# A WKV recurrence on one Trainium2 core: both ends of a written-out order are placed anew

## The chip, the cores and the metric

The kernel runs on one core of one Trainium2 chip. A core has five engines that follow their own instruction queues: TensorE (PE, matrix products into PSUM), VectorE (DVE), ScalarE (ACT), GpSimd (POOL) and SyncE (SP, used here for transfers only). The metric is the device time of the kernel in microseconds; less is better.

## The reference

For each of 16 sequences and 256 channels a state runs over 2048 time steps. It is kept with a running maximum so that no exponential overflows:

```python
for t in range(seq_len):
    ww = u + kk;      qq = maximum(pp, ww)
    e1 = exp(pp - qq); e2 = exp(ww - qq)
    output[b, t] = (e1 * aa + e2 * vv) / (e1 * bb + e2 + 1e-08)
    ww = pp - w + kk; qq = maximum(ww, kk)
    e1 = exp(ww - qq); e2 = exp(kk - qq)
    aa = e1 * aa + e2 * vv; bb = e1 * bb + e2; pp = qq
```

Inputs: w and u (256), k and v (16 x 2048 x 256), all fp32; the output is 16 x 2048 x 256 fp32.

## The kernel before

Time is cut into 16 chunks of 128 steps (c = 0 to 15), the batch into 4 groups of 4 sequences. One group in one chunk is a *pair* n = 4c + p, 64 in all; its k and its v are 512 KB each, its output too. Within a chunk everything is a product with a triangular matrix over time, so TensorE does the sums over time and the state is handed over from chunk to chunk by a short chain on small tiles.

A pair goes through these steps. The engine is in brackets, then the line of the program; q is 0 or 1.

- LK, LV (GpSimd's or SyncE's transfers, L108, L111, L115): loads of k and v. RK (VectorE or GpSimd, L194) copies k to the matmul type, CV (L214) casts v to bf16.
- R q (TensorE, L201, 4 products) and L q (TensorE, L207, 2 products) build the logarithms in one of two PSUM buffers X[0], X[1]; X q (ScalarE, L210) takes their exponential into a ring of 11 pairs, EZR.
- TV (VectorE, L219) multiplies by v. S (TensorE, L246, 8 products) sums over time into TOT.
- DEN (TensorE, L323, 12 products into X) and NUM (the same into a buffer of its own, or into X for the odd ones of the last eight pairs) give the denominator and numerator. LN (ScalarE, L335) and INV (ScalarE, L340) turn the denominator into its inverse, MUL (VectorE, L355) makes the output, ST (SyncE, L368, L361) and SQ store it.

After the S of a chunk's four pairs comes the chain of the state: CS (VectorE, L252, copies the sums), TU (TensorE, L259, turns them into TOT's other columns), SL (ScalarE, L263, logarithm), FR and OF (VectorE, L268 to L276), SW (ScalarE, L282), CH (VectorE, L286, L289), SS (VectorE, L296), TK (TensorE, L303, turns back into TURN), BK (VectorE, L307, copies it). DEN and NUM of the chunk's pairs need BK. SN (L279) and KP (L299) hand two tiles to the next chunk.

The order is written out by the program itself. Each step gets a place, a number: by default the pair's number plus a constant of the table P, in which pair n's output follows about 10 pairs behind its input. The table AT gives single steps a place of their own. At each turn the step with the lowest place whose predecessors are written and whose buffer is free is written; every engine then does its own instructions in that order, and the waits between engines follow from the tiles.

```python
ops[name] = dict(place=AT.get(key, place), fn=fn, args=args, after=list(after), take=take, give=give, mode=mode)
...
todo = sorted(ops, key=lambda x: ops[x]["place"])
```

Fillers: ahead of some TensorE steps a number of products with zeros into TURN is written (`zeros`, L149). Before the first step there are 26. Table Z0 counts them for the steps whose number is 0 and Z for all others; none is written between a TK and its BK, as BK reads TURN. With "L": 1 each L has one.

```python
if o["mode"] and not quiet:
    zeros(P["Z0" if name[-1] < FILL else "Z"].get(name[0], 0))
quiet = quiet and name[0] != "BK" or name[0] == "TK"
```

Buffers that matter here: X[0] and X[1], shared by R/L/X and by DEN/LN; one buffer for NUM; two for the inverse; 4 and 5 for k, 4 for v, 2 for its cast; 8 for the output.

Of the kernel before, what the change touches and what calls it, by code (L numbers as in the profile page):

```python
# [15 lines left out]
def kernel(  # L16
# [37 lines left out]
    FILL = 1  # L54
# [4 lines left out]
         "R": [-0.795, -7.965],  # L59
         "OUT": {"DEN": [-0.47, -0.155, -0.55, -0.495], "LN": [-11.935, -9.86, -0.84, -6.17], "INV": [-13.87, -8.32, -4.99, -5.82], "NUM": [-0.105, 0.155, 0.11, -5.15], "MUL": [1.115, 0.345, 0.895, 1.035], "ST": [-5.05, 7.26, 1.245, 7.765], "SQ": [-3.365, 6.69, -2.4, 8.84]},  # L60
         "TAIL": {"DEN": -4.36, "LN": -16.54, "INV": 3.8, "NUM": -0.31, "MUL": 4.39, "ST": 14.35, "step": 2.989, "SQ": 26.08},
         "Z0": {"L": 1, "S": 3, "DEN": 0, "NUM": 6, "TK": 47, "TU": 17, "R": 12},
         "Z": {"DEN": 0, "L": 1, "NUM": 0, "TK": 4, "S": 0, "TU": 1, "R": 0}}

    AT = {"INV 55": 69.0, "SL 15": 69.1, "LN 56": 69.2, "SW 15": 75.7, "FR 15": 69.3}

    consts = ctx.enter_context(tc.tile_pool(name="consts", bufs=1))
    kpool = ctx.enter_context(tc.tile_pool(name="kpool", bufs=NK))
# [63 lines left out]
    Z = consts.tile([128, 192], BF16, tag="Z", name="Z")  # L132
# [14 lines left out]
    def zeros(m, first=False):  # L147
        for j in range(m):
            K(PE.matmul(TURN[:, 0:192], Z[:, 0:128], Z, start=first, stop=True, skip_group_check=True))  # L149
# [40 lines left out]
    X = [psx.tile([128, 2, D], F32, tag=f"X{a}", name=f"X{a}") for a in range(2)]  # L190
# [31 lines left out]
    AS, D1, L1, A0, FR, BC, A2 = range(7)  # L222
# [88 lines left out]
    RD, NUM, OT = {}, {}, {}  # L311
# [66 lines left out]
    def step(name, place, fn, args=(), after=(), take=None, give=(), mode=0):  # L378
        key = name if isinstance(name, str) else " ".join(map(str, name))
        ops[name] = dict(place=AT.get(key, place), fn=fn, args=args, after=list(after), take=take, give=give, mode=mode)  # L380

# [51 lines left out]
    while todo:  # L433
        for name in todo:
            o = ops[name]
            if all(x not in ops or "done" in ops[x] for x in o["after"]) and (xs if o["take"] == "X" else free.get(o["take"], 1)):
                break
        else:
            raise AssertionError(todo[:9])
        todo.remove(name)  # L440
        args = list(o["args"])
        if o["take"] == "X":
            held[name] = xs.pop(0)
            args.append(held[name])
        elif o["take"]:
            free[o["take"]] -= 1
        elif name[0] == "L":
            args.append(held[("R",) + name[1:]])
        for g in o["give"]:
            if g == "X":  # L450
                x = held[("DEN", name[1]) if name[0] == "LN" else ("NUM", name[1]) if name[0] == "MUL" else ("R",) + name[1:]]
                xs.append(x)
                args.append(x)
            else:
                free[g] += 1
        if o["mode"] and not quiet:
            zeros(P["Z0" if name[-1] < FILL else "Z"].get(name[0], 0))
        quiet = quiet and name[0] != "BK" or name[0] == "TK"
        o["fn"](*args)
        o["done"] = True  # L460
# [30 lines left out]
```

## Time and profile before

| | |
|---|---|
| median of 3 runs | 289.46 us (288.67 to 289.91) |
| the profiled execution | 289.20 us, span 287.5 us |
| TensorE busy | 271.6 us, 94% |
| ScalarE busy | 258.6 us, 90% |
| VectorE busy | 246.9 us, 86% |
| GpSimd busy | 176.4 us, 61% |
| fillers (L149) | 319 products, 11% of the chain that ended last |
| moved | 101.2 MB, 67.12 read and 33.55 written, 350 GB/s over the span |

Busy time counts an engine's instructions from start to modelled end; products overlap, so a busy TensorE need not be at its peak. What an engine waited for stands in brackets behind the first instruction after the wait. Times in the rows are microseconds from the start of the span.

### The profile page before, as it was taken

How to read it: one execution, taken by the hardware profiler on the slowest of the kernel's cores; microseconds unless marked ns; L12 is line 12 of the kernel's file. 1: busy time of each engine (PE TensorE's matmuls, PEld its weight loads, DVE VectorE, ACT ScalarE, POOL GpSimd, SP SyncE). 2: the span in 40 equal slices, each digit the busy share in tenths (PEclk: the TensorE clock that was granted, in tenths of full speed). 3: DMA queues.
4: the chain of work that ended last, by engine and by line, in shares of the span. 5: the costliest groups of instructions: out<-in, count | busy, mean ns of one | idle time of the engine just before them, and what ended most of it. 6: DMA issues, size and time to landing. Idle time of an engine off the chain costs nothing.

```text
span 287.5 us, 8058 instructions
## 1 busy us (share of the span) xinstructions
PE 271.6 (94%) x3263; PEld 139.2 (48%) x3263; DVE 246.9 (86%) x422; ACT 258.6 (90%) x291; POOL 176.4 (61%) x219
## 2 busy tenths in 40 slices
PE   7989999999999999999999999999999999998860
PEld 6535744454545545454545545454545545454530
DVE  4685879989897979989898989989898989889861
ACT  1776399999999999999999999999999999998991
POOL 8256458575767687575767687575767685421320
PEclk9999999999999999999999999999999999999997
DMA  6999999999999999999999999999999999985896
GB/s 206 348 354 346 347 348 313 384 369 390 374 394 381 383 393 372 391 382 393 355 392 388 389 387 382 394 385 395 370 380 374 389 394 387 347 237 177 235 278 179
DMA packets 58669, 101.20 MB, mean 352 GB/s; under 512 B 5152, under 2 KB 43688, under 8 KB 58632
## 3 DMA queue, kind: packets, MB, share of 16 engines
q0 software_dynamic: 21200, 65.42, 65.5%
q1 hardware_dynamic: 37280, 35.14, 36.4%
q8 instruction: 25, 0.41, 0.6%
q10 hardware_dynamic: 152, 0.14, 0.1%
q14 instruction: 12, 0.10, 0.1%
HBM read 67.12 MB, written 33.55 MB: 350 GB/s over the span
## 4 chain that ended last, share of the span: by engine, by line
PE 81%; ACT 6%; DMA 4%; DVE 4%; issue 2%; SPq 1%; DVEq 0%; ACTq 0%
PE X L207 20%; PE X L323 15%; PE num L323 12%; PE X L201 12%; PE TURN L149 11%; PE TOT L246 7%; DMA ot<-in_v_dram 4%; ACT rd L335 3%; PE TOT L259 2%; DVE ot L355 2%; ACT rd L340 2%; DVE EZR L219 1%; ACT EZR L210 1%; PE TURN L303 1%; SPq L115 1%
## 5 line engine op out<-in xcount | busy, mean ns | idle before, releaser
L210 ACT ACTIVATE EZR<-X 128x1024 bf16<-128x1024 f32 x128 | 126.9, 1014 | 14.4 <-PE X L207 14.2
L214 POOL CAST vb<-vr 128x1024 bf16<-128x1024 f32 x54 | 56.4, 1044 | 69.3 <-DVE EZR L219 67.5
L219 DVE TENSOR_TENSOR EZR<-EZR,vb 128x2048 bf16<-128x2048 bf16 x64 | 77.8, 1219 | 0.4 <-ACT EZR L210 0.2
L355 DVE TENSOR_TENSOR ot<-num,rd 128x1024 f32<-128x1024 f32 x60 | 73.3, 1221 | 3.9 <-ACT rd L340 3.6
L340 ACT ACTIVATE rd<-rd 128x1024 f32<-128x1024 f32 (+1 forms) x65 | 68.0, 1046 | 2.0
L335 ACT ACTIVATE rd<-X 128x1024 f32<-128x1024 f32 (+1 forms) x65 | 65.8, 1012 | 2.3 <-PE X L323 0.7
L149 PE MATMUL TURN<-Z 128*128 128x192 bf16 x319 | 55.2, 259 | 1.4 <-DVE Z L133 1.4
L201 PE MATMUL X<-WU,CO 64*64 64x512 bf16 x512 | 51.9, 390 | 0.9 <-DVE WU L176 0.6
L149 PEld LDWEIGHTS <-Z 128*128 128x128 bf16 x319 | 28.4, 100 | 48.6 <-issue 47.1
L115 POOL DMA_DIRECT2D vr<-in_v_dram x61 | 46.3, 759 | 6.7 <-DVE vb L214 5.9
L207 PE MATMUL X<-kr,NLE 128*128 128x512 f32 x128 | 45.6, 438 | 0.0
L207 PE MATMUL X<-kr,NLZ 128*128 128x512 f32 x128 | 45.5, 437 | 0.0
L108 POOL DMA_DIRECT2D kf<-in_k_dram x53 | 40.1, 756 | 0.0
L194 DVE CAST kr<-kf 128x1024 fp32r<-128x1024 f32 x39 | 31.6, 839 | 4.0 <-DMA kf<-in_k_dram 4.0
L201 PEld LDWEIGHTS <-CO 64*64 64x64 bf16 x512 | 15.7, 105 | 31.1 <-issue 26.3
L323 PE MATMUL X<-EZR,S 64*64 64x512 bf16 x256 | 26.2, 394 | 1.7 <-ACT rd L335 1.0
L323 PE MATMUL X<-cb,Id 64*64 64x512 bf16 x256 | 25.9, 376 | 0.0
L323 PE MATMUL X<-EZR,Id 64*64 64x512 bf16 x256 | 25.9, 376 | 0.0
L323 PE MATMUL num<-EZR,SN 64*64 64x512 bf16 x240 | 24.3, 386 | 1.1 <-DVE ot L355 1.1
L246 PE MATMUL TOT<-EZR,OH 128*32 128x256 bf16 x512 | 23.7, 277 | 1.3 <-DVE EZR L219 1.3
L323 PE MATMUL num<-cb,IdN 64*64 64x512 bf16 x240 | 24.0, 376 | 0.0
L323 PE MATMUL num<-EZR,IdN 64*64 64x512 bf16 x240 | 23.9, 376 | 0.0
(69 smaller groups left out, 269.3 us busy)
## 6 DMA issues: line engine op xcount, KB each, us to landing
vr<-in_v_dram POOLq DMA_DIRECT2D x61, 512.0 KB, 7.7
kf<-in_k_dram POOLq DMA_DIRECT2D x53, 512.0 KB, 8.5
out_dram<-ot SPq DMA_DIRECT2D x64, 256.0 KB, 10.0
out_dram<-ot SPq DMA_DIRECT2D x116, 128.0 KB, 10.1
kr<-in_k_dram POOLq DMA_DIRECT2D x8, 512.0 KB, 8.8
ot<-in_k_dram SPq DMA_DIRECT2D x3, 512.0 KB, 5.9
ot<-in_v_dram SPq DMA_DIRECT2D x3, 512.0 KB, 10.0
out_dram<-ot POOLq DMA_DIRECT2D x11, 128.0 KB, 3.4
```

What stands on the lines that cost most here:

```text
L115: K((SP if n < BYSP else POOL).dma_start(out=vr, in_=rows_of(v, n)))
L149: K(PE.matmul(TURN[:, 0:192], Z[:, 0:128], Z, start=first, stop=True, skip_group_check=True))
L201: K(PE.matmul(X[a][o:o + HS, i, :].rearrange("p (n d) -> p n d", n=2), CO[r:r + HS, q, :], WU[r:r + HS, :].unsqueeze(1).broadcast_to([HS, ...
L207: K(PE.matmul(X[a][:, i, :], (NLE, NLZ)[q], km[:, i, :], start=False, stop=True, skip_group_check=True))
L210: K(SC.activation(ez(n)[:, q, 1], X[a], ACT.Exp))
L214: K((DVE if n < EARLY else POOL).tensor_copy(vb, VR.pop(n)))
L219: K(DVE.tensor_mul(ez(n)[:, :, 0], ez(n)[:, :, 1], vb.unsqueeze(1).broadcast_to([128, 2, 2, D])))
L246: K(PE.matmul(t[32 * j:32 * j + 32, 0:256], OH[:, s:s + 32], ez(n)[:, 0, 1 - q, i, 256 * x:256 * x + 256], start=p == 0 and x == 0, stop=p ...
L323: K(PE.matmul(out_tile[o:o + HS, i, :], left, right, start=s == 0, stop=s == 2, tile_position=(r, o), skip_group_check=True))
L335: K(SC.activation(RD[n][:, i], X[a][:, i], ACT.Ln, scale=RS))
L340: K(SC.activation(RD[n][:, i], RD[n][:, i], ACT.Exp, scale=-1.0))
L355: K(DVE.tensor_mul(o.rearrange("p (i n) d -> p i (n d)", i=2)[:, i], NUM[n][:, i], RD[n][:, i]))
```

## The change

The tables alone change. AT now gives places to nearly all steps of pairs 50 to 63 and to the state's steps of chunks 12 to 15 (loads, stores, RK and CV keep theirs, but for the few named below), and to some thirty steps of pairs 0 to 12. Z0 is cut from 47 to 8 ahead of TK 0, from 17 to 2 ahead of TU 0 and from 12 to 6 ahead of R 0 0 and R 1 0. A table ZAT sets 4 fillers ahead of DEN 0, TU 1 and R 0 11. In all 319 fillers become 271.

```diff
-         "Z0": {"L": 1, "S": 3, "DEN": 0, "NUM": 6, "TK": 47, "TU": 17, "R": 12},
+         "Z0": {"L": 1, "S": 3, "DEN": 0, "NUM": 6, "TK": 8, "TU": 2, "R": 6},
...
-    AT = {"INV 55": 69.0, "SL 15": 69.1, "LN 56": 69.2, "SW 15": 75.7, "FR 15": 69.3}
+    AT = {"R 0 50": 48.908, "L 0 50": 39.3462, "X 0 50": 45.2, "R 1 50": 43.3225, "L 1 50": 41.2788,
...
+          "INV 63": 106.9287,
+          "NUM 63": 101.791, "MUL 63": 73.9425, "TU 0": 5.01, "FR 0": 5.02, "SW 0": 6.2, "TK 0": 7.205,
+          "CV 7": 6.4, "TV 5": 5.1, "S 4": 5.3, "S 5": 7.195, "TV 6": 6.3, "S 6": 7.21, "S 7": 8.1, "CH 0": 6.32,
+          "SS 0": 6.33, "BK 0": 7.21, "CV 6": 5.2, "TV 7": 7.3, "KP 0": 8.6, "TV 8": 8, "R 0 6": 5.0,
+          "R 0 8": 7.19, "R 0 9": 7.9, "CS 1": 8.2, "TU 1": 8.3, "SN 0": 8.15, "FR 1": 8.95, "CV 9": 8.0,
+          "SW 1": 9.6, "RK 11": 9.1}
+
+    ZAT = {"DEN 0": 4, "TU 1": 4, "R 0 11": 4}
...
-            zeros(P["Z0" if name[-1] < FILL else "Z"].get(name[0], 0))
+            zeros(ZAT.get(" ".join(map(str, name)), P["Z0" if name[-1] < FILL else "Z"].get(name[0], 0)))
```

What this does to the queues, in words (numbers in brackets are fillers):

- TensorE at the start, before: L 1 6, (17) TU 0, R/L 7, (47) TK 0, S 4, S 5, R/L 8, S 6, R/L 9, S 7, R/L 10, TU 1, DEN 0, (6) NUM 0, R 0 11. After: L 1 6, (2) TU 0, S 4, R/L 7, R/L 8, S 5, (8) TK 0, S 6, R/L 9, S 7, (4) TU 1, R/L 10, (4) DEN 0, (6) NUM 0, (4) R 0 11. The L of pairs 8 to 10 get their one filler each, since BK 0 is now written before them.
- VectorE at the start: TV 5 moves from behind KP 0 to behind OF 0, followed by CV 6 and TV 6, then CH 0 and SS 0; BK 0 moves from behind CS 1 to behind CV 7; RK 12 moves behind SN 1. ScalarE: SL 0 goes between the two X of pair 6, SW 0 ahead of X of pair 7, SL 1 ahead of X of pair 10, SW 1 behind INV 0. GpSimd: RK 11 goes ahead of CV 10.
- TensorE at the end: S 50 goes behind L 1 53, S 52 and S 53 behind DEN 44, S 54 ahead of DEN 46, S 55 behind DEN 47; S 56 to S 59 stand together behind DEN 51, which stands behind DEN 50; S 60 and S 61 go behind NUM 53; NUM 52 goes behind L 1 62; DEN 58 ahead of NUM 56, DEN 59 ahead of NUM 58, and DEN 60 and 61 take X[0] instead of X[1].
- VectorE at the end: TV 53 ahead of CS 12, TV 54 ahead of CH 12, TV 59 ahead of MUL 49, CS 14 ahead of MUL 50, TV 62 ahead of MUL 52, TV 63 ahead of BK 14, MUL 56 ahead of SS 15. ScalarE: SW 11 and SW 13 one X earlier, LN 51 and INV 51 ahead of the X of pair 61, SW 14 ahead of both X of pair 63, SL 15 ahead of INV 55. GpSimd: CV 55 ahead of RK 55, CV 59 ahead of LK 63.
- SyncE's order stays.

44 rows, old and new, of the table AT are left out of this document.

## The prediction

> **What bounds the kernel now.** I read the page's first line and its row of TensorE's clock, a table of stretches (start:end, length, busy time of PE, PEld, DVE, ACT and POOL, clock, DMA share, GB/s), and then the order of time on each engine at both ends (start, us, engine, line, tile, count, idle time before and what ended it).
>
> ```profile
> span 287.5 us, 8058 instructions
> ...
> PEclk9999999999999999999999999999999999999997
> ...
> 25.17:40.92 15.75, 15.75 (x161) 10.46 (x160) 11.91 (x23) 9.16 (x12) 7.89 (x11) 1.00 1.27 348
> ...
> 50.00:250.00 200.00, 199.67 (x2445) 98.17 (x2437) 185.25 (x295) 196.87 (x223) 137.53 (x156) 1.00 1.04 384
> 250.00:262.50 12.50, 11.36 (x153) 5.82 (x151) 10.18 (x19) 12.37 (x15) 3.60 (x5) 1.00 0.81 229
> 262.50:281.20 18.70, 13.72 (x217) 7.67 (x216) 14.55 (x22) 17.11 (x21) 5.46 (x9) 1.00 0.80 232
> ```
>
> Between 50 and 250 us TensorE is busy for 199.67 of 200 us, so whatever it reaches earlier at 50 us it keeps to the end of that stretch; ScalarE, with 196.87, can make up about 3 us of delay over the whole stretch and no more. Before 41 us TensorE only looks busy: its work there holds the filler products. After 250 us ScalarE carries the time (12.37 of 12.50, then 17.11 of 18.70), and its idle time there, 0.13 and 1.59 us, is all that a better order at that end can win.
>
> **The start: what the fillers cost.** Steps are named as in the section on the kernel.
>
> ```profile
> 1.37 4.82 PE L149 MATMUL TURN<-Z 128*128 128x192 bf16 x38 [1.37 <-DVE Z L133]
> ...
> 18.13 0.40 PE L246 MATMUL TOT<-EZR,OH 128*32 128x256 bf16 x6 [0.86 <-DVE EZR L219]
> ...
> 25.17 1.58 PE L149 MATMUL TURN<-Z 128*128 128x192 bf16 x17
> 26.58 0.61 PE L259 MATMUL TOT<-Sel,ts 128*128 128x96 f32 x4
> 27.12 0.41 PE L201 MATMUL X<-WU,CO 64*64 64x512 bf16 x4
> ...
> 29.07 4.05 PE L149 MATMUL TURN<-Z 128*128 128x192 bf16 x47
> 32.96 0.39 PE L303 MATMUL TURN<-Id,CB 128*128 128x128 bf16 x4
> ...
> 40.92 0.41 PE L323 MATMUL X<-EZR,S 64*64 64x512 bf16 x4
> ...
> 42.96 0.39 PE L201 MATMUL X<-WU,CO 64*64 64x512 bf16 x4
> ```
> ```profile
> 16.25 0.69 DVE L214 CAST vb<-ot 128x1024 bf16<-128x1024 f32 x1 [0.66 <-DMA ot<-in_v_dram]
> ...
> 28.65 0.20 DVE L268 TENSOR_TENSOR U<-U 128x64 f32<-128x64 f32 x1
> ...
> 29.69 0.19 DVE L276 TENSOR_SCALAR U<-U 128x64 f32<-128x64 f32 x1
> 30.58 0.29 DVE L286 TENSOR_TENSOR TB<-TOT,G 128x128 f32<-128x128 f32 x1 [0.70 <-ACT G L282]
> ...
> 31.55 0.33 DVE L296 TENSOR_TENSOR CB<-AB,G 128x128 bf16<-128x128 f32 x1
> ...
> 41.15 1.14 DVE L194 CAST kr<-kf 128x1024 fp32r<-128x1024 f32 x1 [1.40 <-DMA kf<-in_k_dram]
> ```
>
> The 12 fillers fewer ahead of R 0 0 and R 1 0 bring nothing: VectorE waits at 16.25 for the third load of v, and S 1 at 18.13 for VectorE, and neither depends on them. Everything up to 25.17 therefore stands at its old time. From there I lay the new order out with the durations of the rows (a filler 1.41 / 17 = 0.083 us; TU 0.54; one R with its L 1.0, two of them lying between 27.12 and 29.07; an X 1.02; frames and offsets 28.65 to 29.88, with overlap 1.15; CH and SS 30.58 to 31.80, 1.2) and 0.05 to 0.1 us for each hand-over between engines (the product that released 18.13 began at 16.86 and took 1.22).
>
> ```profile
> 24.33 2.05 ACT L210 ACTIVATE EZR<-X 128x1024 bf16<-128x1024 f32 x2 [0.33 <-PE X L207]
> 27.23 0.28 ACT L263 ACTIVATE U<-TOT 128x128 f32<-128x128 f32 x1 [0.84 <-PE TOT L259]
> ...
> 30.19 0.36 ACT L282 ACTIVATE G<-U 128x192 f32<-128x192 f32 x1
> ```
>
> - TU 0 after 2 fillers: 25.34 to 25.88, 1.24 earlier. SL 0, now between the two X of pair 6, runs at 25.98 instead of 27.23, so X 1 6 slides to 27.2. S 4, put behind TU 0, has to wait for SL 0 (both use the bank of TOT): 26.3 to 26.6. R and L of pair 7 end at 28.65.
> - FR 0 and OF 0 run 26.35 to 27.5, SW 0 at 27.6 (before 30.19), X 0 7 and X 1 7 until 28.85 and 29.87. R 0 8 waits 0.3 us for that buffer; L 1 8 ends at 31.0.
> - VectorE: TV 5, CV 6, TV 6 until 30.4, CH 0 and SS 0 until 31.65. S 5 at 31.0, 8 fillers, TK 0 at 32.0 (before 32.96), S 6 until 32.66.
> - New wait: BK 0 is now issued ahead of pair 9, so the filler in L 0 9, which writes the bank that BK 0 reads, waits until BK 0 is through at 33.15 (0.15 us of TensorE; L 0 9 and all of TensorE's queue stand behind it). Pair 9 ends at 34.86, S 7 at 35.2, TU 1 waits for CS 1 until 35.7, pair 10 ends at 38.33.
> - DEN 0, behind 4 fillers: 38.66 against 40.92. With 6 fillers, NUM 0 and the 4 new fillers R 0 11 comes at 41.0 against 42.96: 1.96 us earlier.
>
> **The start: what the loads allow.** The loads are taken in, one per about 1.5 us, whatever the engines do.
>
> ```profile
> 20.86 0.74 POOL L111 DMA_DIRECT2D kr<-in_k_dram x1 [2.50 <-PE X L207]
> ...
> DMA to landing us min/median/max: 8.2/8.2/8.2
> ...
> 29.77 0.76 POOL L108 DMA_DIRECT2D kf<-in_k_dram x1
> ...
> DMA to landing us min/median/max: 11.4/11.4/11.4
> ...
> 39.72 1.04 POOL L214 CAST vb<-vr 128x1024 bf16<-128x1024 f32 x1 [1.83 <-DMA vr<-in_v_dram]
> 40.70 1.04 POOL L194 CAST kr<-kf 128x1024 fp32r<-128x1024 f32 x1
> ```
>
> The two landing lines belong to the issue above each: k of pair 8 lands at 29.06, k of pair 12 at 41.17, with four pairs, or eight loads, between them (12.1 / 8 = 1.5 us). L 0 8 is wanted at 29.3, so 0.25 us is left there; pair 9 (32.1) and pair 10 (35.1) have more. RK 12 is the close one. VectorE waited for it until 41.15 before and will again, since the load cannot come sooner, and TV 9, MUL 0, CH 1 and SS 1 are queued behind it; TensorE waits for TV 9 in S 9. RK 12 took 1.14 us beside GpSimd's cast at 40.70; other casts of the group took 0.69:
>
> ```profile
> L194 DVE CAST kr<-kf x39: 681/686/1402, 41.1 to 245.1; 128x1024 fp32r<-128x1024 f32 x39
> ```
>
> At 1.14, TV 9 ends at 43.45, S 9 and then NUM 1 (behind MUL 0) wait, and 1.5 us are left of the 1.96. At 0.69, TV 9 ends at 43.0 while S 8 begins at 43.07, and nothing waits: 1.9. In the new order GpSimd does RK 11 ahead of CV 10, so its casts would end by 40.8. I take 1.8.
>
> The Trainium skill (SBUF — State Buffer, "SBUF: two separate sides") says that VectorE and GpSimd take turns at one shared pair of ports and that the later one is blocked until the earlier is through. By that rule RK 12, alone, would take the short time, and the start would win the full 1.9; the row of 1.14 beside a GpSimd cast agrees.
>
> So the start is worth -1.8 us (-1.4 to -2.0), and TensorE, which has no gap from there to 250 us, hands it on.
>
> **The end: moved steps without gain.** S 50 and S 54 only change places with products that take as long. Two places matter.
>
> ```profile
> 220.09 0.41 PE L323 MATMUL num<-EZR,SN 64*64 64x512 bf16 x4
> ...
> 222.78 0.67 PE L246 MATMUL TOT<-EZR,OH 128*32 128x256 bf16 x16
> ...
> 222.38 1.00 ACT L210 ACTIVATE EZR<-X 128x1024 bf16<-128x1024 f32 x1
> ...
> 220.51 0.23 DVE L268 TENSOR_TENSOR U<-U 128x64 f32<-128x64 f32 x1 [0.77 <-ACT U L263]
> ```
>
> S 52 and S 53 (0.66 us, the row at 222.78) move from behind L 1 55 to behind DEN 44, where NUM 44 began at 220.09. There they must wait for SL 12, whose result is out at 220.51: 0.4 us of TensorE idle. R 0 55 slips by 1.0, X 0 55 from 222.38 to 222.87, and ScalarE, full from there, is 0.4 to 0.5 us late; DEN 45 comes at 223.9 instead of 223.44. ScalarE's idle time in the steady part, 3.1 us in 200, gives back about 0.25 in the 16 us of one chunk at most: +0.2 to +0.5, taken as +0.4.
>
> ```profile
> 256.82 1.02 ACT L335 ACTIVATE rd<-X 128x1024 f32<-128x1024 f32 x1
> ...
> 263.61 0.28 ACT L263 ACTIVATE U<-TOT 128x128 f32<-128x128 f32 x1 [0.67 <-PE TOT L259]
> 264.40 1.03 ACT L335 ACTIVATE rd<-X 128x1024 f32<-128x1024 f32 x1 [0.51 <-PE X L323]
> ...
> 268.74 1.03 ACT L335 ACTIVATE rd<-X 128x1024 f32<-128x1024 f32 x1
> ...
> 281.18 0.69 DVE L355 TENSOR_TENSOR ot<-X,rd 128x512 f32<-128x512 f32 x1 [0.45 <-ACT rd L340]
> ```
>
> The second place is everything from TK 13 on. S 56 to S 59 stand in one block behind DEN 51, and LN 51 and INV 51 before the X of pair 61. From LN 50 to LN 53 ScalarE does the same operations in another order, so LN 53 stays at 256.82 except for new waits. Laid out as above, in the old times: DEN 52 comes 0.1 us after ScalarE is ready for LN 52, L 0 63 and L 1 63 (now behind NUM 52) 0.2 and 0.15 us after it is ready for their X. LN 53 starts at 257.3. INV 53 ends at 259.35; behind it VectorE does MUL 53 and TV 63 (1.14 each) until 261.75, then S 63, BK 14 with CS 15 until 262.7, and TU 15 brings SL 15 to 263.5. ScalarE is through LN 54, INV 54 and LN 55 at 262.4, so its wait of 1.1 us stays; but LN 56 then follows INV 55 without the second wait, 0.51, that stands at 264.40. With SW 15 among them, LN 57 starts at 267.0 and LN 58 at 269.05 instead of 268.74. From there LN and INV alternate as before: each DEN now waits for the LN before it on one buffer (0.65 us and two hand-overs, hidden under an INV of 1.04), SS 15, put behind MUL 56, still gives TK 15 a microsecond before LN 59 needs DEN 59, and the last product (281.18) and its store follow as now. So +0.3, with -1.2 (both waits of ScalarE gone) and +1 (SL 15 a microsecond later) as the bounds.
>
> **The sum.** The profiled execution took 289.20 us (span 287.5 and 1.7 around it), 0.26 under the median 289.46, less than the three runs differ. 289.2 - 1.8 + 0.4 + 0.3 = 288.1.
>
> **The rivals.**
>
> *The end wins too.* ScalarE's two waits close because SL 15 arrives while there is still an LN to do. For it: the 1.2 us at 263.61 and 264.40 are real. Against: the chain from X 1 63 to TU 15 is no shorter. Then 289.2 - 1.9 - 1.0 = 286.3 to 287.3; I give it 0.22.
>
> *The start is not handed on.* The loads take the gain back: k of pair 12 comes no sooner, and the kernel in its steady part moves 384 GB/s, more than the 348 of the start, so that TensorE, ahead of the loads, would wait for later ones. It decides if any load after pair 12 has less than 1.8 us to spare. Against: TensorE idles 0.33 us in 200, and the loads follow buffers that come free sooner too. Then 289.2 + 0.7 = 289.9; 0.17.
>
> *TensorE loses its full clock.* The fillers of the start keep it busy: 48 of 319 are gone, most from one block of 3.9 us. In the trace the first 38 fillers took 4.82 us, while 47 later took 3.89 (29.07 to 32.96), so a slow rate exists here; the row of the clock, nines throughout, shows it at no later time. If it came back between 27 and 33 us for some 3 us of work, that work would take twice as long: 288.1 + 3 = 291.1. It decides from a gap as long as those fillers were; the new order, as laid out, has no gap over 0.3 us. With a like loss at the end 0.11.
> The Trainium skill (TensorE: Matmul & The Clock Gate, "HAM oscillation — how this bites in real kernels") warns of idle gaps over about 3.4 us. By that rule the change would be slower only if S 5 or TK 0 came several microseconds later than I place them; no row of before shows such a gap.
>
> **How the numbers follow.** Forecast 0.50, with 287.2 to 289.2 as its own range; the rivals 0.22, 0.17 and 0.11. The range 286.4 to 290.4 leaves out the clock's case and the edge of the first. A change of 0.5% is 1.45 us, about what a measurement of this kernel can tell from none: faster means below 288.0. Nearly half of the forecast and all of the first rival lie there: 0.45. Slower (above 290.9) is the clock's case and a little: 0.13. Between them 0.42.
>
> **What would show it.** After: the first L 259 (TU 0) near 25.3, DEN 0 near 38.7, R 0 11 near 41.0, a wait of VectorE for k until about 41.15, and then a steady part that runs 1.4 to 2.0 us ahead; a TensorE wait of 0.4 us ahead of S 52; LN 53 about 0.5 us later than the steady part would put it. I am wrong at the start if DEN 0 comes after 40 or the shift is gone by 60 us; wrong at the end if the time from L 1 54 to the last INV changes by other than +0.2 to +1.0.

## The result and the profile after

| | before | after |
|---|---|---|
| median | 289.39 us (288.6 to 290.06, 12 runs) | 288.6 us (287.63 to 289.59, 12 runs) |
| ratio to before | | 0.9963, 95% interval [0.9949, 0.9978] |
| profiled execution | 289.2 us, span 287.5 us | 288.6 us, span 286.9 us |

By the ratio the kernel is 0.37% faster, about 1.1 us; the two medians lie 0.8 us apart. In the profiled execution SL 12 came 1.84 us earlier, where -1.8 was forecast; the end took 0.85 us of it back (1.36 lost in chunks 12 and 13, 0.51 won behind them), and the stretch behind the last product 0.4 us more.

The page of the changed kernel, its first line and the row of TensorE's clock; nines again from the first slice on:

```profile
span 286.9 us, 7963 instructions
...
PEclk9999999999999999999999999999999999999997
```

The start, TensorE's order of time in the changed kernel (start, us, engine, line, tile, count, idle time before and what ended it; the lines are 51 higher than before, so L200 is the filler, L252 R, L258 L, L297 S, L310 TU, L354 TK and L374 DEN and NUM):

```profile
24.02 0.41 PE L252 MATMUL X<-WU,CO 64*64 64x512 bf16 x4
...
25.12 0.61 PE L310 MATMUL TOT<-Sel,ts 128*128 128x96 f32 x4
26.10 0.40 PE L297 MATMUL TOT<-EZR,OH 128*32 128x256 bf16 x8 [0.37 <-ACT U L314]
...
28.71 0.41 PE L252 MATMUL X<-WU,CO 64*64 64x512 bf16 x4 [0.16 <-ACT EZR L261]
...
31.10 0.83 PE L200 MATMUL TURN<-Z 128*128 128x192 bf16 x8
31.77 0.39 PE L354 MATMUL TURN<-Id,CB 128*128 128x128 bf16 x4
...
32.94 0.24 PE L200 MATMUL TURN<-Z 128*128 128x192 bf16 x1
...
35.57 0.69 PE L310 MATMUL TOT<-Sel,ts 128*128 128x96 f32 x4
...
38.57 0.41 PE L374 MATMUL X<-EZR,S 64*64 64x512 bf16 x4
...
41.15 0.41 PE L252 MATMUL X<-WU,CO 64*64 64x512 bf16 x4
```

TU 0, S 4, TK 0, TU 1, DEN 0 and R 0 11 stand within 0.25 us of where the prediction laid them. About 0.2 us of the lead isn't the change's own: R 1 6, still ahead of the steps that moved, already starts at 24.02, where before it was

```profile
24.23 0.41 PE L201 MATMUL X<-WU,CO 64*64 64x512 bf16 x4
```

VectorE's wait for the third load of v had ended 0.22 us earlier in this execution (16.03 and 16.25). Such differences come by themselves: in e_end, below, which has the old start, SL 0 ran 0.66 us earlier than before. From R 1 6 to R 0 11 the new order takes 17.13 us instead of 18.73, so it won 1.6 us here, not 1.84. ScalarE's and VectorE's rows there:

```profile
25.77 0.28 ACT L314 ACTIVATE U<-TOT 128x128 f32<-128x128 f32 x1 [0.62 <-PE TOT L310]
...
27.39 0.38 ACT L333 ACTIVATE G<-U 128x192 f32<-128x192 f32 x1 [0.42 <-DVE U L327]
```
```profile
39.87 1.06 DVE L330 COPY U<-U 128x64 f32<-128x64 f32 x1
41.24 0.81 DVE L245 CAST kr<-kf 128x1024 fp32r<-128x1024 f32 x1 [0.31 <-DMA kf<-in_k_dram]
```

RK 12 (41.24) again starts when its k lands, and takes 0.81 us instead of 1.14. SN 1 (39.87), a small copy that takes 0.2 us elsewhere, took 1.06 beside GpSimd's cast CV 10, which began at 39.82; nobody waited for it.

The end, by engine, around chunk 12 and from LN 53 on (L261 X, L319 to L327 FR and OF, L340 the two scans of CH, L347 SS, L386 LN; L265 on GpSimd is CV 56):

```profile
218.68 0.62 PE L297 MATMUL TOT<-EZR,OH 128*32 128x256 bf16 x16 [0.24 <-ACT U L314]
...
226.07 0.40 PE L354 MATMUL TURN<-Id,CB 128*128 128x128 bf16 x4 [0.23 <-DVE CB L347]
...
230.70 0.41 PE L374 MATMUL X<-EZR,S 64*64 64x512 bf16 x4 [0.55 <-ACT EZR L261]
```
```profile
221.00 1.02 ACT L261 ACTIVATE EZR<-X 128x1024 bf16<-128x1024 f32 x1 [0.38 <-PE X L258]
...
227.62 1.03 ACT L386 ACTIVATE rd<-X 128x1024 f32<-128x1024 f32 x1 [0.59 <-PE X L374]
...
256.30 1.03 ACT L386 ACTIVATE rd<-X 128x1024 f32<-128x1024 f32 x1
...
262.51 0.28 ACT L314 ACTIVATE U<-TOT 128x128 f32<-128x128 f32 x1 [1.18 <-PE TOT L310]
...
263.63 1.02 ACT L386 ACTIVATE rd<-X 128x1024 f32<-128x1024 f32 x1
...
267.75 1.01 ACT L386 ACTIVATE rd<-X 128x1024 f32<-128x1024 f32 x1
```
```profile
218.79 0.91 DVE L319 TENSOR_TENSOR U<-U 128x64 f32<-128x64 f32 x1
...
223.32 1.33 DVE L340 TENSOR_TENSOR_SCAN AB<-G,TB 128x96 f32<-128x96 f32 x2
...
224.80 1.21 DVE L347 TENSOR_TENSOR CB<-AB,G 128x128 bf16<-128x128 f32 x1
```
```profile
224.76 1.05 POOL L265 CAST vb<-vr 128x1024 bf16<-128x1024 f32 x1
```

X 0 55 (221.00) was at 222.38 before: it is ahead by 1.38 and no longer by 1.84, as the forecast had it. But LN 46 (227.62) is a second loss: ScalarE waits 0.59 us for DEN 46, which waits for TK 12, which waits for SS 12. Three operations of VectorE's chain, FR 12, a scan of CH 12 and SS 12, took 0.6 to 0.9 us longer than they do elsewhere. How far that was from the usual, by groups of all 16 chunks (duration in ns: least/median/most), first before, then after:

```profile
L289 DVE TENSOR_TENSOR_SCAN AB<-G,TB x32: 330/345/359, 30.9 to 266.8; 128x96 f32<-128x96 f32 x32
L296 DVE TENSOR_TENSOR CB<-AB,G x16: 329/332/348, 31.5 to 267.2; 128x128 bf16<-128x128 f32 x16
```
```profile
L340 DVE TENSOR_TENSOR_SCAN AB<-G,TB x32: 323/345/1076, 30.7 to 265.7; 128x96 f32<-128x96 f32 x32
L347 DVE TENSOR_TENSOR CB<-AB,G x16: 315/332/1214, 31.3 to 267.4; 128x128 bf16<-128x128 f32 x16
```

No such operation was slow before; after, one scan and one SS were. SS 12 starts 0.04 us after GpSimd's cast CV 56 (224.80 and 224.76) and ends 0.2 us after it (226.01 and 225.81).

The Trainium skill (SBUF — State Buffer, "SBUF: two separate sides") says that of a GpSimd operation and a VectorE operation that need the shared ports, the one that starts first keeps them for its whole length. SS 12 and FR 12 (beside the cast RK 55, 218.58 to 219.62) agree.

The last product and the landing of the last store (ScalarE's queue), after and then before:

```profile
280.18 0.69 DVE L406 TENSOR_TENSOR ot<-X,rd 128x512 f32<-128x512 f32 x1 [0.45 <-ACT rd L391]
```
```profile
out_dram<-ot ACTq DMA_DIRECT2D x1, 128.0 KB, 4.8
```
```profile
out_dram<-ot ACTq DMA_DIRECT2D x1, 128.0 KB, 3.9
```

The last product is 1.00 us earlier (281.18 before). ScalarE's last store lands 0.9 us later behind its issue, the stretch from the last product to the end of the span is 0.4 us longer, and so the span is only 0.6 us shorter.

### The profile page after: what moved, and what is told of

Same layout as the page of the kernel before. It is cut to its first block, busy times and chain, and to the rows that moved or that the text cites. A ratio compares the mean times of both kernels' runs of the same rounds, so it can differ in the third digit from the quotient of the medians.

```text
span 286.9 us, 7963 instructions
## 1 busy us (share of the span) xinstructions
PE 268.8 (94%) x3215; PEld 136.5 (48%) x3215; DVE 249.6 (87%) x422; ACT 258.7 (90%) x291; POOL 179.7 (63%) x219
## 4 chain that ended last, share of the span: by engine, by line
PE 67%; ACT 14%; DVE 8%; DMA 4%; issue 3%; SPq 1%; DVEq 0%
PE X L258 16%; PE X L374 14%; PE num L374 11%; PE X L252 9%; PE TURN L200 8%; ACT rd L386 6%; PE TOT L297 5%; ACT rd L391 4%; DMA ot<-in_v_dram 4%; ACT EZR L261 3%; DVE EZR L270 2%; PE TOT L310 2%; DVE ot L406 1%; PE TURN L354 1%; DVE vb L265 1%
## 5 line engine op out<-in xcount | busy, mean ns | idle before, releaser
L261 ACT ACTIVATE EZR<-X 128x1024 bf16<-128x1024 f32 x128 | 126.5, 1014 | 11.9 <-PE X L258 11.9
L265 POOL CAST vb<-vr 128x1024 bf16<-128x1024 f32 x54 | 59.6, 1104 | 66.2 <-DVE EZR L270 65.6
L386 ACT ACTIVATE rd<-X 128x1024 f32<-128x1024 f32 (+1 forms) x65 | 65.7, 1011 | 2.5 <-PE X L374 0.9
L200 PE MATMUL TURN<-Z 128*128 128x192 bf16 x271 | 53.6, 266 | 1.7 <-DVE Z L184 1.4
L252 PE MATMUL X<-WU,CO 64*64 64x512 bf16 x512 | 51.9, 390 | 1.0 <-DVE WU L227 0.6
L200 PEld LDWEIGHTS <-Z 128*128 128x128 bf16 x271 | 25.1, 103 | 50.3 <-issue 48.7
L258 PE MATMUL X<-kr,NLE 128*128 128x512 f32 x128 | 45.6, 437 | 0.0
L258 PE MATMUL X<-kr,NLZ 128*128 128x512 f32 x128 | 45.5, 436 | 0.0
L245 DVE CAST kr<-kf 128x1024 fp32r<-128x1024 f32 x39 | 30.9, 821 | 3.3 <-DMA kf<-in_k_dram 3.3
L252 PEld LDWEIGHTS <-CO 64*64 64x64 bf16 x512 | 16.0, 104 | 31.6 <-issue 26.6
L374 PE MATMUL X<-EZR,S 64*64 64x512 bf16 x256 | 26.2, 395 | 4.3 <-ACT rd L386 2.0
L374 PE MATMUL X<-cb,Id 64*64 64x512 bf16 x256 | 25.9, 376 | 0.0
L374 PE MATMUL X<-EZR,Id 64*64 64x512 bf16 x256 | 25.9, 375 | 0.0
L297 PE MATMUL TOT<-EZR,OH 128*32 128x256 bf16 x512 | 23.1, 276 | 1.4 <-DVE EZR L270 0.8
L374 PE MATMUL num<-EZR,SN 64*64 64x512 bf16 x240 | 24.3, 385 | 0.0
L374 PE MATMUL num<-cb,IdN 64*64 64x512 bf16 x240 | 24.0, 376 | 0.0
L374 PE MATMUL num<-EZR,IdN 64*64 64x512 bf16 x240 | 24.0, 376 | 0.0
```

What stands on the lines that cost most here:

```text
L252: K(PE.matmul(X[a][o:o + HS, i, :].rearrange("p (n d) -> p n d", n=2), CO[r:r + HS, q, :], WU[r:r + HS, :].unsqueeze(1).broadcast_to([HS, ...
L258: K(PE.matmul(X[a][:, i, :], (NLE, NLZ)[q], km[:, i, :], start=False, stop=True, skip_group_check=True))
L261: K(SC.activation(ez(n)[:, q, 1], X[a], ACT.Exp))
L265: K((DVE if n < EARLY else POOL).tensor_copy(vb, VR.pop(n)))
L374: K(PE.matmul(out_tile[o:o + HS, i, :], left, right, start=s == 0, stop=s == 2, tile_position=(r, o), skip_group_check=True))
L386: K(SC.activation(RD[n][:, i], X[a][:, i], ACT.Ln, scale=RS))
```

## The experiments

Times are medians, each beside runs of the kernel before on the same chip; 0.995 means 0.5% faster than it. The steps of one profiled execution of each, as differences of the starts of ScalarE's SL and LN and of VectorE's last product, in microseconds:

| kernel | SL 12 at | to LN 46 | LN 46 to 50 | LN 50 to 58 | to the last product | to the span's end |
|---|---|---|---|---|---|---|
| before | 220.19 | 8.23 | 16.18 | 24.14 | 12.44 | 6.3 |
| after | 218.35 | 9.27 | 16.50 | 23.63 | 12.43 | 6.7 |
| after, once more (a_again) | 218.59 | 8.86 | 16.51 | 23.63 | 12.43 | 6.7 |
| e_start | 218.25 | 8.57 | 16.17 | 24.14 | 12.44 | 6.2 |
| e_start2 | 218.54 | 8.56 | 16.18 | 24.13 | 12.44 | 6.3 |
| e_end | 219.47 | 9.28 | 16.51 | 23.65 | 12.42 | 7.1 |
| e_fill | 220.87 | 8.21 | 16.17 | 24.14 | 12.44 | 6.9 |
| e_place | 222.30 | 9.28 | 16.50 | 23.62 | 12.42 | 6.2 |
| t_s52 | 218.52 | 9.32 | 16.51 | 23.63 | 12.42 | 6.2 |
| t_tv53 | 218.78 | 8.73 | 16.51 | 23.63 | 12.42 | 6.6 |
| t_cv55 | 218.69 | 9.28 | 16.50 | 23.62 | 12.42 | 6.8 |
| t_c12old | 218.69 | 8.22 | 18.00 | 23.65 | 12.42 | 6.2 |
| t_c13old | 218.55 | 8.21 | 16.33 | 23.62 | 12.42 | 6.3 |

### The start alone

```diff
     AT = {"INV 55": 69.0, "SL 15": 69.1, "LN 56": 69.2, "SW 15": 75.7, "FR 15": 69.3,
+          "TU 0": 5.01, "FR 0": 5.02, "SW 0": 6.2, "TK 0": 7.205, "CV 7": 6.4, "TV 5": 5.1,
...
+          "SW 1": 9.6, "RK 11": 9.1}
+    ZAT = {"DEN 0": 4, "TU 1": 4, "R 0 11": 4}
```
(Z0 as in the changed kernel: TK 8, TU 2, R 6.)

> The start's tables alone (places of pairs 0 to 12, the cut of Z0, ZAT); pairs 50 to 63 as before. Theory A (the start wins 1.8 us, the steady part hands it on, the end gives some back): 289.4 - 1.8 = 287.6, faster than the changed kernel by about 1; R 0 11 near 41.1 and the last product near 281.18 - 1.8 = 279.4. Rival B (the loads take the gain back by the end, and the changed kernel's gain comes from its end): 289.4. Rival C (the two ends need each other): no change or slower.

287.93 us, ratio 0.9935 [0.9911, 0.9959]: -1.9 us. The start alone is worth what the prediction put on it, and the changed kernel as a whole brought less, 1.1 us, though their intervals just overlap. In its trace the start alone loses 0.34 us between SL 12 and LN 46, in the old order of steps. There VectorE's RK 56 waits for its k:

```profile
216.47 1.06 DVE L201 CAST kr<-kf 128x1024 fp32r<-128x1024 f32 x1 [1.24 <-DMA kf<-in_k_dram]
```

Before, the same step waited 0.33 us and started at 217.50: it gained 1.0 us where the engines had gained 1.9, and then took 1.06 us (1.48 in e_start2) beside a cast of GpSimd's. In t_c13old, below, it started at 216.19, took 0.69 us, and nothing was lost. This is the rival of the loads at the size of a third of a microsecond, and it is at work before chunk 12 too. Between 55 us and SL 12, eight of the nine traces with the start's tables and its fewer fillers (the table above; the changed kernel's first execution is the ninth) lose 0.33 to 0.36 us in one place, and e_fill in two. In each such place an RK of VectorE had waited 0.73 us or more for its k, the MUL behind it came late, and TensorE waited 0.36 to 0.38 us for the buffer of NUM. Where an RK waited 0.69 us or less, nothing was lost. In the changed kernel's second execution the place is this:

```profile
135.10 1.53 DVE L245 CAST kr<-kf 128x1024 fp32r<-128x1024 f32 x1 [0.77 <-DMA kf<-in_k_dram]
```
```profile
137.82 0.41 PE L374 MATMUL num<-EZR,SN 64*64 64x512 bf16 x4 [0.38 <-DVE ot L406]
```

### The end alone

AT as in the changed kernel for pairs 50 to 63 and chunks 12 to 15; the start's places, Z0 and ZAT as before.

> The end's places alone (pairs 50 to 63, chunks 12 to 15); start and fillers as before. Theory A: the end gives back what the changed kernel's trace lacks of the start's 1.84 us, the last product comes 0.7 to 1.0 us later than before: 290.1 to 290.4. Rival B: faster, 288.5. By the trace of the changed kernel the loss sits in chunk 12 (about 1 us: 0.4 ahead of S 52, 0.6 ahead of LN 46) and chunk 13 (0.3), and about 0.5 of it is won back between LN 55 and LN 58.

290.1 us, ratio 1.0011 [0.9991, 1.0031]: nothing, or 0.3 us lost. From SL 12 to the last product its trace takes 0.87 us more than before, in the same places as the changed kernel: +1.05 until LN 46, +0.33 until LN 50, -0.49 until LN 58.

### The fillers without the places, and the places without the fillers

```diff
-         "Z0": {"L": 1, "S": 3, "DEN": 0, "NUM": 6, "TK": 47, "TU": 17, "R": 12},
+         "Z0": {"L": 1, "S": 3, "DEN": 0, "NUM": 6, "TK": 8, "TU": 2, "R": 6},
```
(That line alone, AT as before and no ZAT.)

> Only the cut of Z0 (47 to 8 ahead of TK 0, 17 to 2 ahead of TU 0, 12 to 6 ahead of R 0 0 and R 1 0); all places as before. TK 0 then waits for SS 0, which waits for the load of v of pair 6 and comes at 31.6: TensorE has nothing to do for about 3 us. Theory A (the clock stays full): TensorE gets to R 0 8 only 0.4 us earlier, since S 5 has to wait for TV 5; 289.0. Rival C (the idle stretch takes TensorE's clock to half for some 3 us of work): 290 to 291, with L behind 32 us taking twice as long.

291.0 us, ratio 1.0045 [1.0015, 1.0075]: +1.3 us, slower than before. The rows show the rival "TensorE loses its full clock" at work. TensorE's order of time, the stretch from 32 to 36 us (length, busy time of PE, PEld, DVE, ACT, POOL, clock, DMA share, GB/s) and the page's row of the clock:

```profile
28.39 0.83 PE L151 MATMUL TURN<-Z 128*128 128x192 bf16 x8
31.46 0.61 PE L305 MATMUL TURN<-Id,CB 128*128 128x128 bf16 x4 [2.23 <-DVE CB L298]
32.00 1.32 PE L248 MATMUL TOT<-EZR,OH 128*32 128x256 bf16 x16
```
```profile
32.00:36.00 4.00, 4.00 (x37) 1.58 (x36) 3.97 (x6) 1.04 (x2) 1.49 (x2) 0.67 1.23 353
```
```profile
PEclk9999799999999999999999999999999999999996
```

TensorE sat idle for 2.23 us, the clock fell to a mean of 0.67 for about 4 us, and 16 products of S took 1.32 us instead of 0.62. The 39 fillers taken from TK 0 (39 x 0.083 = 3.2 us) had covered that time, and the old order has nothing else for TensorE to do in it. In this execution nothing is left of what the missing fillers had won: TK 0 comes 1.5 us earlier than before (31.46 and 32.96), R 0 8 0.6 (33.24 and 33.83), R 1 8 and SL 1 at the same time (34.85 and 34.83; 41.55 and 41.53). From R 0 8 to R 1 8 it takes 1.61 us instead of 1.00, which is the clock; of the 0.7 us that S 4 and S 5 took longer a part is S 5's, which had to wait for TV 5 until 32.65 at any clock. The 0.7 us by which SL 12 is late are two waits for k as above, and the stretch behind the last product adds 0.6, so the trace doesn't show the +1.3 as the clock's. The other executions point to it: of the twelve, eight with a mean granted clock of 0.983 to 0.988 took 289.9 to 291.3 us, and four with 0.972 to 0.978 took 291.9 to 293.7; the kernel before was granted 0.987 or more in all of its executions on that chip.

The Trainium skill (TensorE: Matmul & The Clock Gate, "HAM oscillation — how this bites in real kernels") speaks of gaps over about 3.4 us; here one of 2.23 us was enough, and the measurement decides.

The other half is AT as in the changed kernel with the old Z0 and no ZAT.

> All places of the changed kernel with the old fillers (Z0 47, 17, 12; no ZAT). Theory A: TU 0 comes 1.24 us later than in the changed kernel, and the 47 fillers, now ahead of a TK 0 that could run at once, cost their 39 x 0.083 = 3.2 us, less 0.9 for the fillers of ZAT: DEN 0 and all behind it 3.4 to 3.6 us later than in the changed kernel, 292.1. Rival (fillers fill time in which TensorE waits anyway): 288.6.

292.57 us, ratio 1.009 [1.0065, 1.0116]: +2.6 us on before and +4.0 on the changed kernel (SL 12 at 222.30 and 218.35). Each half of the start loses, and both together win 1.9 us: the places put S 4, R and L of pairs 7 and 8 and S 5 into the time in which the fillers kept TensorE busy, and only then can the fillers go.

### What chunk 12 lost

S 52 and S 53 back behind L 1 55 (their two entries of AT taken out):

```diff
-          "S 52": 53.6213,
...
-          "S 53": 45.2725,
```

> The changed kernel with S 52 and S 53 alone put back behind L 1 55. Theory A (the end's loss in chunk 12 is paid where the changed kernel's trace shows ScalarE waiting: 0.38 us ahead of X of pair 55, 0.59 ahead of LN 46): the 0.38 goes; 288.6 - 0.4 = 288.2 beside a changed kernel at 288.6. Rival D (ScalarE loses the same time elsewhere, since VectorE's steps are still in the new order): 288.6.

288.63 us, ratio 0.9974 [0.9954, 0.9994], no better than the changed kernel. From SL 12 to LN 46 nothing is won (9.32). ScalarE waits for the chain now:

```profile
227.84 1.03 ACT L379 ACTIVATE rd<-X 128x1024 f32<-128x1024 f32 x1 [0.66 <-PE X L367]
```

TV 53 taken out of AT as well, which puts it back behind SN 12 and GpSimd's CV 55 back behind LK 59:

> As the one before, and TV 53 put back behind SN 12, with which CV 55 goes back behind LK 59. Theory A (in the changed kernel GpSimd's cast CV 55 and the casts beside it stretch VectorE's small chain steps in chunk 12: the scan 1.33 instead of 0.61, SS 1.21 instead of 0.33, so TK 12 waits 0.23 and LN 46 0.59): the second wait goes too; 287.8. Rival E (the wait ahead of LN 46 comes from S 54 ahead of DEN 46, 0.33 us of products): 288.2.

288.84 us, 0.9978 [0.9959, 0.9997]. Chunk 12 gets 0.54 us back (8.73; 0.13 against the second execution of the changed kernel), the time none: SL 12 itself came later in this execution (218.78), behind one of the waits for k. FR 12 takes its usual 0.23 us again, one scan is still slow, and SS 12, which begins 0.03 us ahead of GpSimd's cast CV 56, takes 0.33 us; here the cast is the longer one:

```profile
225.57 0.33 DVE L340 TENSOR_TENSOR CB<-AB,G 128x128 bf16<-128x128 f32 x1
```
```profile
225.60 1.19 POOL L258 CAST vb<-vr 128x1024 bf16<-128x1024 f32 x1
```

GpSimd's cast alone, CV 55 back behind LK 59 and everything else as in the changed kernel:

```diff
+    AT = {"CV 55": 54.8,
```

> The changed kernel with one step put back: GpSimd's cast CV 55 stands behind LK 59 again instead of ahead of RK 55. Theory A (the time lost in chunk 12 beyond the 0.4 us of S 52 comes from GpSimd: CV 55 waits there for its v, RK 55 and the five loads behind it come 2 to 3 us later, and its casts stretch VectorE's chain of the state): RK 55 starts near 216.3 instead of 218.6 to 219.2, no operation of the chain takes over 0.6 us, SL 12 to LN 46 takes 8.6 to 8.7 us instead of 8.9 to 9.3, and the time is 288.0 to 288.4 us, ratio 0.994 to 0.996. Theory B (S 52's wait and the order of TensorE and ScalarE cost it): SL 12 to LN 46 stays at 8.9 to 9.3 and the ratio at 0.9964.

288.51 us, 0.9966 [0.9951, 0.9982], and 9.28 us: no gain, and my guess of the cause fails. RK 55 comes earlier again (217.48 instead of 218.58), but the chain is as slow. VectorE's rows and GpSimd's cast:

```profile
223.71 1.33 DVE L333 TENSOR_TENSOR_SCAN AB<-G,TB 128x96 f32<-128x96 f32 x2
...
225.19 1.17 DVE L340 TENSOR_TENSOR CB<-AB,G 128x128 bf16<-128x128 f32 x1
```
```profile
225.10 1.07 POOL L258 CAST vb<-vr 128x1024 bf16<-128x1024 f32 x1
```

The cast here is CV 56, which stands at its old place in GpSimd's order. What has moved is the chain: with TV 54 ahead of CH 12, SS 12 falls on that cast. The changed kernel run once more shows it from the other side; there SS 12 started 0.22 us ahead of the cast, took its usual time, and LN 46 waited 0.18 us instead of 0.59, though the scan in FR 12 took 1.07 us beside the cast RK 55:

```profile
225.12 0.34 DVE L347 TENSOR_TENSOR CB<-AB,G 128x128 bf16<-128x128 f32 x1
```
```profile
225.34 1.05 POOL L265 CAST vb<-vr 128x1024 bf16<-128x1024 f32 x1
```

> The changed kernel itself, on the chip of the two kernels beside it, so that the three can be compared. Both theories: 288.6 us, ratio to the kernel before 0.996 to 0.997.

288.46 us, 0.9964 [0.9944, 0.9984]: the same time as in the first measurement.

### The old order in chunks 12 and 13

The start's tables with all of the end's entries that concern inputs up to pair 55, outputs up to LN 49 and the state of chunk 12 taken out:

> The changed kernel with all of the old order up to L 1 58 (pairs 50 to 55 and chunk 12), the new one behind it. Theory A: the start's 1.8 to 1.9 us and the gain behind LN 55 (about 0.4 less 0.3 in chunk 13) without the loss of chunk 12: 287.4 to 287.6, about 1.0 faster than the changed kernel. Rival D (what is won there is lost in chunk 13, ScalarE being full): 288.4.

289.22 us, 0.9999 [0.9983, 1.0015]: slower than the changed kernel. Chunk 12 is as before (8.22), but LN 46 to LN 50 takes 18.00 us. That is an order which neither kernel has: S 55, its entry taken out, came to stand directly behind NUM 46, where both kernels have it behind L 1 57, and TV 55, for which it waits, is as late as ever. TensorE waits for VectorE, and ScalarE for TensorE:

```profile
229.31 0.40 PE L280 MATMUL TOT<-EZR,OH 128*32 128x256 bf16 x6 [1.12 <-DVE EZR L253]
```
```profile
230.76 2.04 ACT L244 ACTIVATE EZR<-X 128x1024 bf16<-128x1024 f32 x2 [1.73 <-PE X L241]
```

On top of this kernel, 18 fillers fewer at the start (TK 4, NUM 0, none at DEN 0 and R 0 11) and RK 12 behind TV 9:

> As the one before, with 18 more of the start's fillers gone (none ahead of DEN 0, NUM 0 and R 0 11, 4 ahead of TK 0) and RK 12 behind TV 9, so that S 9 no longer stands behind the load of k of pair 12. TensorE then reaches R 0 11 1.2 us earlier, at 40.0. Theory A (the start is bound by TensorE's queue and by RK 12, and the steady part hands on what it wins): another 0.7 to 1.1 less, 286.4 to 286.9. Rival B (the loads are next: later RK and CV wait for theirs): no less than the kernel before it, 287.5. Rival C (fewer fillers, half clock): 288 or more.

289.82 us, 1.0015 [0.9992, 1.0037]. It has the same order at S 55, so what the fewer fillers do isn't settled.

The start once more, beside the changed kernel, and then with the end's order from behind S 55 only:

> The start's tables alone once more, beside the changed kernel on one chip. Theory A (the end's part costs about 1 us net): 287.5 to 288.1 us, ratio 0.993 to 0.995, and 0.5 to 1.1 us below the changed kernel. Theory B (the first batch's 0.9935 was chance, the end is worth nothing either way): 288.6 us, equal to the changed kernel within 0.3 us.

287.82 us, 0.993 [0.9908, 0.9953].

> The start's tables, and of the end's tables only what orders the instructions behind the sum of pair 55: TensorE's S 55, the chain of chunks 12 and 13 and GpSimd's casts up to pair 58 stand as in the kernel before. Theory A (the changed end loses 1.3 us in chunks 12 and 13 and wins 0.5 us from LN 50 to LN 58): 287.0 to 287.5 us, ratio about 0.992, 0.5 us below the start alone, with 8.2 us from SL 12 to LN 46 and 8.0 us from LN 46 to SL 13 as before. Theory B (the 0.5 us is only the time handed back that the earlier chunks had lost, a queue that had been held up): the same time as the start alone, about 287.9 us, with LN 50 to LN 58 at 24.1 us as before instead of 23.6.

288.07 us, 0.9945 [0.9922, 0.9968]. In its trace chunk 12 is as before (8.21), with no slow operation in the chain:

```profile
222.72 0.61 DVE L318 TENSOR_TENSOR_SCAN AB<-G,TB 128x96 f32<-128x96 f32 x2
...
223.48 0.34 DVE L325 TENSOR_TENSOR CB<-AB,G 128x128 bf16<-128x128 f32 x1
```

and LN 50 to LN 58 keeps the 0.5 us won (23.62), so the gain there is the tail's own and not a debt handed back. Its profiled execution is the shortest (span 285.4 us). In the medians it doesn't stand apart from the start alone: the intervals overlap almost wholly. The intervals of both lie below 1; against the changed kernel, e_start2 was 0.64 us faster on the same chip, with intervals that just overlap, so that the end costs time is likely and not shown by the medians.

## Why the prediction was right or wrong

Forecast 288.1 us, measured 288.6: -0.37% where -0.47% was expected, inside the range and inside the 0.5% that counts as no change.

- **What bounds the kernel.** Right in the main. In the first execution TensorE keeps to SL 12 what it had gained by 56 us (SL 2 is 1.79 us earlier, SL 12 1.84); in the second 1.92 us shrink to 1.60 at one wait for k.
- **The fillers at the start.** Right in each step: TU 0 at 25.12 (25.34 forecast), S 4 waits for SL 0, R 0 8 waits 0.16 us (0.3), TK 0 at 31.77 (32.0), the filler of L 0 9 behind BK 0 at 32.94 (33.15), TU 1 at 35.57 (35.7), DEN 0 at 38.57 (38.66), R 0 11 at 41.15 (41.0). Term -1.8, measured -1.9 by the start alone. Part of the match in the one trace is luck: 0.2 of its 1.84 us were there before the moved steps, and counted from R 1 6 the lead at R 0 11 is 1.6 us where 1.96 was laid out.
- **What the loads allow.** Right at the start: RK 12 starts at 41.24, takes 0.81 us and holds nobody up. By the rule of the Trainium skill weighed there (SBUF — State Buffer, "SBUF: two separate sides") RK 12 was to be short without a GpSimd cast beside it; it had none, and 0.81 us instead of 1.14 agrees. Behind the start the loads did take a part, the 0.33 to 0.36 us above, for which the sum had no term.
- **"Moved steps without gain", chunk 12.** The place was right, the size wrong. S 52's move cost what was worked out (X 0 55 0.46 us late, 0.49 forecast), with a wait of TensorE of 0.24 us where 0.4 was laid out. The step that failed is the one that took nothing else there to be late, +0.4: TV 53 and TV 54 ahead of VectorE's chain put its FR, scan and SS beside GpSimd's work, they took up to 1.2 us instead of 0.2 to 0.35, and TK 12 and DEN 46 waited. The term was +0.63 to +1.04 in the two executions. The two delays lie side by side: taking out S 52's alone (t_s52) or the cast's alone (t_cv55) brought nothing, taking out both with TV 53 0.13 to 0.54 us, and the whole old order all of it. What stays open is the scan: it was slow beside GpSimd's load issues in all versions with TV 54 ahead of CH 12, and not beside them in the old order.
- **Chunk 13.** Not in the sum; LN 46 to LN 50 took 0.32 to 0.34 us more in every kernel that had the new order there. The old order has S 55 (0.33 us of products) between L 1 57 and DEN 47, where TensorE would otherwise wait; in the new one TensorE waits 0.55 us ahead of DEN 47 and does S 55 behind it, and LN 47 to LN 48 takes 4.35 us instead of 3.98. With S 55 and the chain of chunk 13 put back (t_c13old) 0.15 of the 0.32 us remain; S 55 alone was not put back.
- **"Everything from TK 13 on", +0.3.** Wrong in sign: -0.51 from LN 50 to LN 58. The waits of 0.1, 0.2 and 0.15 us that I laid out for DEN 52 and L of pair 63 did not come: LN 50 to LN 53 takes 12.18 us, 12.22 before. Of the rest, LN 53 to SL 15 was right, 6.21 us (6.2 forecast, 6.79 before), SL 15's wait stays at 1.18 (1.1), and the second wait, 0.51, is gone; but SL 15 to LN 58, laid out at 5.55 us, took 5.24.
- **The last stores.** "The last product and its store follow as now" failed by 0.4 us: from the last product to the span's end it took 6.7 us instead of 6.3, and ScalarE's last store landed after 4.8 us instead of 3.9. The two don't go together everywhere: with the whole new end the store took 4.3 us in e_place with a stretch of 6.2, and 4.1 in t_tv53 with 6.6. e_fill, with the old end, has 4.5 and 6.9. What ends the span there, and why it varies, stays open.
- **The sum.** -1.84 + 1.04 + 0.32 - 0.51 = -1.0 at the last product (forecast -1.1), by terms of which two were off by half a microsecond and more, against each other; the 0.4 us behind it gives the span's -0.6. From L 1 54 to the last INV the time changed by +0.82 us, inside the +0.2 to +1.0 that the prediction set as its test of the end. That the end's sum came out so near is luck: a loss of 1.36 us where 0.4 was forecast, and a gain of 0.51 where a loss of 0.3 was.
- **The rivals.** "Start is not handed on": not as a whole, but a third of a microsecond of it went to late loads in all but one of the nine traces with the start's tables and its fewer fillers. "The end wins too": its first wait stayed, as argued. "TensorE loses its full clock": not in this kernel, but real in e_fill, from a shorter gap than the 3.9 us I set for it. There the median is +1.3 us and not +3; its one trace shows 0.6 us of the clock's cost in pair 8 and at most 0.7 in S 4 and S 5.

## What to carry to other kernels

Fillers that keep a clock up and an order that leaves nothing else to do are one cost: cut the fillers and move real work into their place in the same step, and measure each half, because each may lose where both win. When an order by hand moves large operations of one engine past a chain of small ones, look up what the other engines, here GpSimd, do at that moment; the chain's length by its usual durations is a lower bound. Two delays that end at the same step can't be told by undoing either alone, and half an undo can make a wait that neither order has.

## What the runs showed of the hardware

- In e_fill a TensorE idle time of 2.23 us was enough for a granted clock of 0.67 over the 4 us behind it.
- VectorE's operations on 128x64 to 128x128 elements, 0.2 to 0.35 us alone, took 0.9 to 1.2 us when they started up to 0.2 us behind a GpSimd cast, and ended 0.1 to 0.2 us after the cast did (FR 12, SS 12, SN 1). In the thirteen traces of the table 29 such operations began 0.01 to 0.52 us behind the start of a cast, with 0.25 us or more of it still to run, and all ended 0.07 to 0.21 us after its end. One that began with a cast, within 0.01 us, took its usual 0.22. SS begun 0.22 us ahead of a cast took 0.34 us, and begun 0.03 us ahead 0.33, with the cast stretched from 1.05 to 1.19.
- The same program's executions differ by whole waits: SL 12 to LN 46 took 9.27 and 8.86 us in two executions of the changed kernel, and before and e_start, which have the same order there, 8.23 and 8.57 us. Differences of 0.3 us in one profiled execution are no verdict on an order.
